# The mixers' gate vector moves from TensorE products to VectorE sums in a flow-matching block

## The chip, the cores and the metric

One Trainium2 chip, one NeuronCore. The metric is the device time of one execution in microseconds; the median of several runs stands for a kernel. TensorE is called PE below, VectorE DVE, ScalarE ACT, GpSimd POOL and SyncE SP, as the profile has them.

## The reference, cut to what matters

The block runs on 256 context tokens and then on 256 latent tokens, with the same weights, in fp32. A modulation comes first: six vectors of 2048 from a conditioning vector.

```python
def _modulation(cond, w, bias):
    m = jax.nn.silu(cond) @ w + bias
    return [a[:, None, :] for a in jnp.split(m, 6, axis=-1)]
...
o_c, ctx_states = _mix(_modnorm(h_c, norm1_g[l], m_c[0], m_c[1]), h_c.shape[1], zero, lp)
o_x, _ = _mix(_modnorm(h_x, norm1_g[l], m_x[0], m_x[1]), GRID_W, ctx_states, lp)
h_x = h_x + m_x[2] * o_x
h_x = h_x + m_x[5] * _swiglu(_modnorm(h_x, norm2_g[l], m_x[3], m_x[4]), ffn_w_gu[l], ffn_w_down[l])
return _rmsnorm(h_x, final_g)
```

`_mix` is a projection into four groups (GLA, gated delta rule, short convolution, RWKV-7), their scans, and one output projection. Vector 2 of the modulation, `m_x[2]`, is the gate on the mixers' output; vectors 3 and 4 are shift and scale of the second norm; vector 5 is the gate on the feed-forward part. Vector 2 is needed first after the output projection, where the residual is formed.

## The kernel before, in words

Sizes: `D` is 2048, `KT` 16 blocks of 128, `T` 256 tokens. A weight tile in fp32 is loaded as `wraw` (128x512, 256 KB; eight buffers shared by all loads of this kind), and `split` (L253) makes a high part `wh` on ACT and a rest `wl` on DVE; three products per block then give nearly fp32 accuracy. A projection (`proj`, L600) takes one 128-wide column tile of `w_in` in four quarters; each quarter is a load of `wraw`, a split and twelve products into one of the two PSUM banks `big`. `spill` (L628) copies a result into `xs` and writes it to memory as `xr_...`, and `fetch` reads it back where a mixer needs it.

The mixers' middle part is written as a list of tokens, `ORDER` (L41): a lower-case token is the context pass, an upper-case token the latent pass. `rw` is an RWKV unit, `gd` a delta-rule head, `gl` a GLA pair; `pr`, `pd`, `pg` are projections that are spilled for them; `sc` is a short convolution, with three projections of its own; `FF` empties the list `feed`, and `YY` ends the RWKV part. Units of two streams run beside each other: RWKV (tiles `rw_...`, `iva...`, banks `ea`, `la`) and the rest (`gd_...`, `ivb...`, banks `eb`, `lb`). A scheduler lays out each engine's order: what is ready goes by priority, which is the place in the program plus the number behind a token; loads under `high_priority()` go ahead of all that isn't. A tile waits for a buffer of its tag; a load that finds no `wraw` free waits until the earliest reader is done. So the projections, which depend on little, fill PE where the scans leave it free.

There are 66 projections in the list. After `YY0` come 24 of them, in the order `PG1` (6), `PG0` (6), `SC0` (3), then `GL0` and `GL1` (none) and `SC2`, `SC3`, `SC1` (9). `YY0` itself (L1465) closes the pools of RWKV, `iva`, `rw` and `rings`, and opens the pool `yp` in their place, with `reuse_waits="tile"`: a tile of `yp` can be written when the RWKV tiles at its address have been read for the last time. `yp` holds 32 tiles of 1 KB a partition (`yH`, `yL`), and then, in order of first use, `g2` (8 KB), `yr`, `ss` and `prt`. RWKV unit 3 of the latent pass (`RW3`) is the last to use the old tiles.

Vectors 2 to 4 of the modulation are formed by `ada_pieces` (L285): 16 pieces and a finish per vector, put into `feed` at L1434 in the order 3, 4, 2. `proj` takes one piece out of `feed` at each even quarter (L610). A piece loads four tiles `wraw` of `ada_w` (L298) and issues sixteen products into the bank `ob`, with the conditioning vector `sc` as stationary operand of 32 columns. For vector 2 the finish (L308) loads the bias, adds it, and writes the gate to `gate_dram`. After the mixers, `gate_bc` (L498) reads it into `g2` on all partitions, and `residual` multiplies with it.

Vector 5 is formed in the feed-forward part in another way: `gate_piece` (L1557) loads a tile, and DVE multiplies it by the scalar `sc[:, kt, 0:1]` and adds it to `gacc`; a product with a matrix of ones sums the partitions.

Of the kernel before, what the change touches and what calls it, by code (L numbers as in the profile page):

```python
# [16 lines left out]
P = 128  # L17
D = 2048
KT = D // P
# [21 lines left out]
ORDER = ("rw0:-50 pd3 pd2:550 pd1 gd0:650 pg0 gd1 pg1:-150 XX0 rw1 gl0 gd3 rw3 gd2:500 gl1:400 "  # L41
         "rw2:-150 PD0 PR0:-200 XX1 GD0:-100 RW0:50 PR1 PD3 PD1:150 RW1 FF0:-100 PR2:350 PR3:-750 "
         "GD1 RW2 PD2:-1100 GD2:200 RW3 YY0:-450 GD3 PG1 PG0:-350 SC0:-250 GL0:50 GL1:-150 "
         "SC2:-3400 SC3:150 SC1").split()
LEVS = (16, 32, 64)

TILES = ([("small", 0)] + [(n, i) for n, k in (
# [109 lines left out]
def _pack_ada(w):  # L157


    a = w.reshape(KT, P, 6, KT, P)  # L160
    first = a[:, :, 0:2].transpose(3, 1, 0, 2, 4).reshape(KT * P, KT * 2 * P)
    later = w[:, 2 * D:5 * D].reshape(KT, P, 3, 4, 4, P).transpose(2, 4, 0, 1, 3, 5).reshape(3 * 4 * KT * P, 512)
    last = w[:, 5 * D:].reshape(KT * P, 4, 512).transpose(1, 0, 2).reshape(4 * KT * P, 512)
    later = np.concatenate([later, last])
    return np.ascontiguousarray(first), np.ascontiguousarray(later)


# [8 lines left out]
def block_kernel(ctx: ExitStack, tc: tile.TileContext, x, cx, ada_first, ada_later, ada_b, w_in, w_early, w_out,  # L176
                 w_gu, w_down, final_g, consts, params, small, out):
    nc = tc.nc
    V, A, G, TE = nc.vector, nc.scalar, nc.gpsimd, nc.tensor
# [8 lines left out]
    def mk(pool, shape, tag, bufs=None, dt=F32):  # L188
        pool = sub.get(tag[:3], pool) if pool is sub.get("mx") else pool
        return pool.tile(list(shape), dt, tag=tag, name=nm(tag), bufs=bufs)  # L190
# [10 lines left out]
    def tt(o, a, b, op, e=None):  # L201
        (e or V).tensor_tensor(out=o, in0=a, in1=b, op=op)  # L202

    def ts(o, a, s1, op0, s2=None, op1=None, e=None):
        if s2 is None:
            (e or V).tensor_scalar(out=o, in0=a, scalar1=s1, scalar2=None, op0=op0)
        else:
            (e or V).tensor_scalar(out=o, in0=a, scalar1=s1, scalar2=s2, op0=op0, op1=op1)

    def stt(o, a, s, b, op0, op1, e=None):  # L210
        (e or V).scalar_tensor_tensor(out=o, in0=a, scalar=s, in1=b, op0=op0, op1=op1)

    def mm(o, l, r, start=True, stop=True):
        return TE.matmul(o, l, r, start=start, stop=stop)  # L214
# [7 lines left out]
    MUL, ADD, SUB, MIN, MAX = ALU.mult, ALU.add, ALU.subtract, ALU.min, ALU.max  # L222
# [7 lines left out]
    ones = mk(keep, [P, P], "ones")  # L230
# [14 lines left out]
    sc = mk(keep, [P, KT, 32], "sc")  # L245
# [4 lines left out]
    def wraw():  # L250
        return mk(wp[0], [P, wp[1]], "wraw", wp[3])
# [31 lines left out]
    gate_dram = mk(dram, [1, D], "gated")  # L283

    def ada_pieces(ci, bank_of, tmp):  # L285

        st = {}

        def run(j, k0):

            if not st:
                st["ps"] = bank_of([P, 512])
            ps, raws = st["ps"], {}
            for kt in (k0 + 1, k0 + 2, k0 + 3, k0):
                with tc.high_priority():
                    raws[kt] = wraw()
                    r0 = (((ci - 2) * 4 + j) * KT + kt) * P
                    nc.sync.dma_start(raws[kt], ada_later[r0:r0 + P, :])  # L298
            with tc.high_priority():
                for kt in range(k0, k0 + 4):  # L300
                    rv = raws[kt].rearrange("p (g c) -> p g c", g=4)
                    for g in range(4):
                        mm(ps[32 * g:32 * g + 32, j * P:(j + 1) * P], sc[:, kt, :], rv[:, g], kt == 0, kt == KT - 1)

        def finish():
            ps = st["ps"]
            row = wraw()
            if ci == 2:  # L308
                G.memset(row, 0.0)
                for g in range(4):  # L310
                    nc.sync.dma_start(row[32 * g:32 * g + 1, :], ada_b[0:1, ci * D + g * 512: ci * D + (g + 1) * 512])
                tt(row, ps, row, ADD)
                for g in range(4):
                    nc.sync.dma_start(gate_dram[0:1, g * 512:(g + 1) * 512], row[32 * g:32 * g + 1, :])
                return
            acopy(row, ps)
            pt = bank_of([P, 4, 4, 32])
            for b in range(4):
                TE.transpose(pt[:, b].rearrange("p a c -> p (a c)"), row[:, b * P:(b + 1) * P], ident)
            t = modB if ci == 3 else modA  # L320
            tt(t[:, 2, :].rearrange("p (g b) -> p g b", b=4), pt[:, :, :, 0].rearrange("p b g -> p g b"),
               pc("adab", ci * 16, 16).rearrange("p (g b) -> p g b", b=4), ADD)
            if ci == 4:
                stt(t[:, 2, :], t[:, 2, :], 1.0, pc("n2g", 0, 16), ADD, MUL)

        return [lambda j=j, k0=k0: run(j, k0) for j in range(4) for k0 in range(0, KT, 4)] + [finish]

    def rstd_of(src, tmp, n):
        junk = mk(tmp, [P, D], "junk", 1)
# [60 lines left out]
    with ExitStack() as st:  # L390
# [37 lines left out]
        acc = [mk(ps0, [P, 2, T], f"acc{i}") for i in range((NE + 1) // 2)]  # L428
# [36 lines left out]
        w = early_weights(0)  # L465
        ins = first_vectors(0)
        for kt in range(KT):
            wh, wl = w
            if kt < KT - 1:
                w = early_weights(kt + 1)  # L470
# [45 lines left out]
    with mix:  # L516
# [78 lines left out]
                L.append(l)  # L595
            return H, L

        feed = []

        def proj(nHL, which):  # L600

            r0 = TIDX[which] * P
            H, L = nHL
            ps = PB([P, T], "big")
            for hf in range(4):
                with tc.high_priority():
                    raw = wraw()
                    nc.sync.dma_start(raw, w_in[r0:r0 + P, hf * 512:(hf + 1) * 512])
                    wh, wl = split(raw, V)
                if hf % 2 == 0:  # L610
                    for f in feed[:1]:
                        f()
                    del feed[:1]
                for k in range(4):
                    kt = hf * 4 + k
                    a, b = wh[:, k * P:(k + 1) * P], wl[:, k * P:(k + 1) * P]
                    mm(ps, a, H[kt], kt == 0, False)
                    mm(ps, a, L[kt], False, False)
                    mm(ps, b, H[kt], False, kt == KT - 1)
            return ps  # L620
# [263 lines left out]
        def finish(stream):  # L884
            if rest[stream]:
                rest[stream]()
                rest[stream] = None
# [542 lines left out]
        bdLM = Ring(rings, "bdLM", [P, 4, 2, 2, 64], 2)  # L1430
        bdKh = Ring(rings, "bdKh", [P, 4, 2, 64], 1)
        bdE = Ring(rings, "bdE", [P, 4, 2, 64], 1)
        for ci in (3, 4, 2):
            feed += ada_pieces(ci, lambda shape: mk(pb, shape, "ob", 1), mx)  # L1434
        nHL = H0, L0
        rg = None
        for tok in ORDER:
            st, _, ofs = tok.partition(":")
            with tc.high_priority(offset=int(ofs)) if ofs else ExitStack():
                c, low = int(st[-1]), st[:2].lower()  # L1440
                s = int(st[0].isupper())
                if low == "pr":
                    park([(n, c) for n in ("r_k", "r_v", "r_r")[:2 + s] if s or (n, c) not in EARLY], s)
                elif low == "pd":
                    park([(n, c) for n in (dkv, dkv + ("d_q", "d_z"))[s] if s or (n, c) not in EARLY], s)
                elif low == "pg":
                    park(gnames[c] + (gmore[c] if s else []), s)
                elif low == "xx":
                    if c == 0:
                        nHL = load_nT()  # L1450
                        smx = t1("rgate")
                        acopy(smx, proj(nHL, ("small", 0)))
                    else:
                        sms[1] = smalls(smx)
                        prg = pcol(nHL, "r_g", 0)
                        rg, tmp = t1("rgate"), t1("gd_k")
                        logsig(rg, prg, tmp)
                        act(rg, rg, AF.Exp)
                elif low == "ff":
                    for f in feed:  # L1460
                        f()
                    del feed[:]
                elif low == "sc":
                    short_conv(c, nHL)
                elif low == "yy":  # L1465
                    finish("a")
                    rws.close()
                    yp = mix.enter_context(tc.tile_pool(name="yp", bufs=1, reuse_waits="tile"))
                    yH, yL = ([mk(yp, [P, T], f"y{n}{i}", 1, F32R) for i in range(16)] for n in "HL")
                    yt += [yH, yL]  # L1470
                else:
                    dict(gd=gd, rw=rw, gl=gl)[low](c, s)
        finish("b")
# [83 lines left out]
    def gate_piece(i):  # L1557
        kt, q = divmod(i, 4)
        raw = mk(narrow[0], [P, 512], "wraw", narrow[3])
        r0 = ((3 * 4 + q) * KT + kt) * P  # L1560
        nc.sync.dma_start(raw, ada_later[r0:r0 + P, :])
        if kt == 0:
            ts(gacc[q], raw, sc[:, 0, 0:1], MUL)
        else:
            stt(gacc[q], raw, sc[:, kt, 0:1], gacc[q], MUL, ADD)

    gate_todo = list(range(4 * KT))
    for f in range(FT):
# [112 lines left out]
```

## Time and profile before

| | |
|---|---|
| median of 3 runs | 1982.04 us (1973.36 to 1990.49) |
| the profiled execution | 1979.17 us |
| its span, first to last instruction | 1977.4 us |
| PE, PE weight load, DVE, ACT, POOL busy | 94%, 82%, 68%, 52%, 8% of the span |
| granted PE clock, mean | 0.983 |
| mixers' part (list of tokens) | about 159 to 1137 us |
| output projection and second norm | about 1118 to 1230 us |

The span is the profiled execution's own; 1.8 us of its time lie outside. Busy times of PE are modelled ends of pipelined products, so the start of one product to the start of the next is the better measure of what one costs.

### The profile page before, as it was taken

Reading aid. Unit: us, or ns where it says so; the run is one execution under the profiler, and the core shown is the slowest. Engines: PE = TensorE matmul, PEld = TensorE weight load, DVE = VectorE, ACT = ScalarE, POOL = GpSimd, SP = SyncE. Lnnn points to the kernel's source line nnn. Section 1 sums busy time; section 2 is a strip of 40 time slices with the busy share of each in tenths; the row PEclk is TensorE's granted clock in tenths of the full one; section 3 lists DMA queues with packets and bytes.
Section 4 is the critical chain, followed back from the end, with each engine's and each line's share of the span. In section 5 each row is a group of like instructions: output and inputs, shape, how many; then the busy total and the mean of one; then the engine's idle time right before and its main releaser. Section 6 shows DMA issues by size and latency. Waiting matters only on the chain.

```text
span 1977.4 us, 36172 instructions
## 1 busy us (share of the span) xinstructions
PE 1858.0 (94%) x13312; PEld 1622.9 (82%) x13312; DVE 1352.5 (68%) x3327; ACT 1020.7 (52%) x2125; POOL 155.0 (8%) x207
## 2 busy tenths in 40 slices
PE   5898899899999999999999998999999999999998
PEld 3777788788888988888999986888888888888886
DVE  3446767888879789899767567986555555555554
ACT  2225555575575655656455555555555545544444
POOL 0001000000001001101010001110010010000000
PEclk6999999899999999999999999999999999999999
DMA  8985877255473431322344665996555555665664
GB/s 332 397 341 199 277 244 238 69 190 176 126 240 106 146 100 61 101 72 86 110 142 143 220 185 173 318 316 212 184 189 184 189 185 187 201 207 193 193 196 153
DMA packets 162081, 374.66 MB, mean 189 GB/s; under 512 B 17896, under 2 KB 43752, under 8 KB 156784
## 3 DMA queue, kind: packets, MB, share of 16 engines
q1 hardware_dynamic: 156288, 368.21, 55.7%
q10 hardware_dynamic: 5616, 4.14, 0.7%
q8 instruction: 104, 1.70, 0.3%
q14 instruction: 73, 0.60, 0.1%
HBM read 360.48 MB, written 11.80 MB: 188 GB/s over the span
## 4 chain that ended last, share of the span: by engine, by line
PE 75%; DVE 9%; DMA 8%; ACT 5%; issue 2%; POOL 0%; SPq 0%; ACTq 0%; DVEq 0%; POOLq 0%
PE acc L214 40%; PE big L214 14%; PE la L214 6%; DMA wraw<-in_ada_later 5%; PE ea L214 5%; PE lb L214 3%; DVE wl L202 3%; PE eb L214 3%; PE ob L214 2%; ACT wh L197 2%; PE pt L214 0%; DMA wraw<-in_x 0%; DMA xin<-in_cx 0%; ACT rw_z L193 0%; DMA wraw<-in_w_in 0%
## 5 line engine op out<-in xcount | busy, mean ns | idle before, releaser
L202 DVE TENSOR_TENSOR wl<-wraw,wh 128x512 fp32r<-128x512 f32 x856 | 570.7, 693 | 370.0 <-ACT wh L197 364.0
L197 ACT ACTIVATE wh<-wraw 128x512 fp32r<-128x512 f32 x856 | 509.9, 625 | 485.9 <-PE acc L214 197.0
L214 PE MATMUL acc<-n,wh 128*128 128x512 f32 x1408 | 492.7, 398 | 3.3 <-ACT wh L197 3.3
L214 PE MATMUL acc<-n,wl 128*128 128x256 f32 x1408 | 383.2, 282 | 1.8 <-DVE wl L202 1.8
L214 PE MATMUL big<-nh,wh 128*128 128x256 f32 x1056 | 311.9, 296 | 4.4 <-ACT xs L197 3.0
L214 PE MATMUL big<-nh,wl 128*128 128x256 f32 x1056 | 311.2, 295 | 0.7 <-DVE wl L202 0.7
L214 PEld LDWEIGHTS acc<-n,wh 128*128 128x128 f32 x1408 | 259.4, 189 | 60.1 <-ACT wh L197 3.6
L214 PE MATMUL big<-nl,wh 128*128 128x256 f32 x1056 | 307.7, 292 | 0.0
L214 PEld LDWEIGHTS acc<-n,wl 128*128 128x128 f32 x1408 | 267.1, 190 | 11.7 <-DVE wl L202 3.3
L214 PEld LDWEIGHTS big<-nh,wh 128*128 128x128 f32 x1056 | 200.9, 190 | 11.3 <-ACT xs L197 3.8
L214 PEld LDWEIGHTS big<-nh,wl 128*128 128x128 f32 x1056 | 200.5, 190 | 4.0 <-issue 2.1
L214 PEld LDWEIGHTS big<-nl,wh 128*128 128x128 f32 x1056 | 200.8, 190 | 2.0 <-issue 1.1
L214 PE MATMUL acc<-wh,hH 128*128 128x512 f32 x352 | 137.6, 391 | 0.0
L214 PE MATMUL acc<-wh,hL 128*128 128x512 f32 x352 | 137.2, 390 | 0.0
L214 PE MATMUL acc<-wl,hH 128*128 128x512 f32 x352 | 137.2, 390 | 0.0
L202 POOL TENSOR_TENSOR hL<-sg,hH 128x256 fp32r<-128x256 f32 x44 | 46.7, 1061 | 452.5 <-ACT hH L197 452.5
L214 PEld LDWEIGHTS acc<-wh,hH 128*128 128x128 f32 x352 | 66.1, 188 | 14.1 <-ACT up L197 0.2
L214 PEld LDWEIGHTS acc<-wl,hH 128*128 128x128 f32 x352 | 66.1, 188 | 13.9 <-DVE wl L202 0.2
L214 PEld LDWEIGHTS acc<-wh,hL 128*128 128x128 f32 x352 | 66.1, 188 | 13.8
L214 PE MATMUL ob<-wraw,sc 128*32 128x128 f32 x1536 | 52.7, 280 | 24.9 <-DMA wraw<-in_ada_later 21.2
L214 PEld LDWEIGHTS ob<-wraw,sc 128*32 128x32 f32 x1536 | 39.9, 111 | 34.2 <-DMA wraw<-in_ada_later 27.6
L202 DVE TENSOR_TENSOR wl<-wr,wh 128x1408 fp32r<-128x1408 f32 x16 | 26.0, 1624 | 43.3 <-ACT wh L197 43.3
(482 smaller groups left out, 3175.3 us busy)
## 6 DMA issues: line engine op xcount, KB each, us to landing
wraw<-in_w_gu SPq DMA_DIRECT2D x174, 512.0 KB, 3.3
wraw<-in_w_in SPq DMA_DIRECT2D x264, 256.0 KB, 3.2
wraw<-in_ada_later SPq DMA_DIRECT2D x256, 256.0 KB, 4.2
wraw<-in_w_down SPq DMA_DIRECT2D x88, 512.0 KB, 4.2
ad<-in_ada_first SPq DMA_DIRECT2D x32, 1024.0 KB, 9.8
wraw<-in_w_out SPq DMA_DIRECT2D x64, 256.0 KB, 2.8
wr<-in_w_early SPq DMA_DIRECT2D x16, 704.0 KB, 6.2
xin<-in_cx SPq DMA_DIRECT2D x2, 1024.0 KB, 7.9
```

The source lines that it names most:

```text
L197: A.activation(o, i, AF.Copy)
L202: (e or V).tensor_tensor(out=o, in0=a, in1=b, op=op)
L214: return TE.matmul(o, l, r, start=start, stop=stop)
```

## The change

The gate vector (2) leaves `ada_pieces`; shift and scale stay there. Its weights are packed in the layout that vector 5 has, in column quarters of 512. A list `late` of 68 pieces (for each of four quarters, 16 of one load and one DVE operation each, and a finish) is put into `feed` at `YY0`, when `yp` is open; from there on `proj` takes a piece at every quarter, not at every second. The accumulator of a quarter is a tile `prt` of `yp`, with two buffers. The finish multiplies by ones into a bank of `big`, loads the bias row, adds and writes 512 elements of `gate_dram`. `ada_sum` is shared with vector 5. `ORDER` gets a last token `FF0`.

```diff
-         "SC2:-3400 SC3:150 SC1").split()
+         "SC2:-3400 SC3:150 SC1 FF0").split()
...
-    later = w[:, 2 * D:5 * D].reshape(KT, P, 3, 4, 4, P).transpose(2, 4, 0, 1, 3, 5).reshape(3 * 4 * KT * P, 512)
-    last = w[:, 5 * D:].reshape(KT * P, 4, 512).transpose(1, 0, 2).reshape(4 * KT * P, 512)
-    later = np.concatenate([later, last])
+    def quarters(lo, hi):
+        return w[:, lo * D:hi * D].reshape(KT * P, 4 * (hi - lo), 512).transpose(1, 0, 2).reshape(-1, 512)
+
+    later = w[:, 3 * D:5 * D].reshape(KT, P, 2, 4, 4, P).transpose(2, 4, 0, 1, 3, 5).reshape(2 * 4 * KT * P, 512)
+    later = np.concatenate([quarters(2, 3), later, quarters(5, 6)])
...
-            if ci == 2:
-                G.memset(row, 0.0)
-                for g in range(4):
-                    nc.sync.dma_start(row[32 * g:32 * g + 1, :], ada_b[0:1, ci * D + g * 512: ci * D + (g + 1) * 512])
-                tt(row, ps, row, ADD)
-                for g in range(4):
-                    nc.sync.dma_start(gate_dram[0:1, g * 512:(g + 1) * 512], row[32 * g:32 * g + 1, :])
-                return
...
+    def ada_sum(acc, raw, kt):
+        if kt == 0:
+            ts(acc, raw, sc[:, 0, 0:1], MUL)
+        else:
+            stt(acc, raw, sc[:, kt, 0:1], acc, MUL, ADD)
+
+    def gate_pieces(bank_of, tmp):
+
+        st = {}
+
+        def piece(q, kt):
+            if kt == 0:
+                st["acc"] = mk(tmp, [P, 512], "prt", 2)
+            with tc.high_priority():
+                raw = wraw()
+                r0 = (q * KT + kt) * P
+                nc.sync.dma_start(raw, ada_later[r0:r0 + P, :])
+            ada_sum(st["acc"], raw, kt)
+
+        def finish(q):
+            ps = bank_of([P, 512])
+            mm(ps, ones, st["acc"])
+            row = wraw()
+            nc.sync.dma_start(row[0:1], ada_b[0:1, 2 * D + q * 512:2 * D + (q + 1) * 512])
+            tt(row[0:1], ps[0:1, :], row[0:1], ADD)
+            nc.sync.dma_start(gate_dram[0:1, q * 512:(q + 1) * 512], row[0:1])
+
+        return [f for q in range(4) for f in [lambda q=q, kt=kt: piece(q, kt) for kt in range(KT)] +
+                [lambda q=q: finish(q)]]
...
-        feed = []
+        feed, late = [], []
...
-                if hf % 2 == 0:
+                if hf % 2 == 0 or late:
...
-        for ci in (3, 4, 2):
+        for ci in (3, 4):
...
                     yt += [yH, yL]
+                    late += gate_pieces(lambda shape: mk(pb, shape, "big", 2), yp)
+                    feed += late
...
-        if kt == 0:
-            ts(gacc[q], raw, sc[:, 0, 0:1], MUL)
-        else:
-            stt(gacc[q], raw, sc[:, kt, 0:1], gacc[q], MUL, ADD)
+        ada_sum(gacc[q], raw, kt)
```

## Rows read from the trace of the kernel before

**Rows 1.** The page's busy time of each engine over the span.
```profile
PE 1858.0 (94%) x13312; PEld 1622.9 (82%) x13312; DVE 1352.5 (68%) x3327; ACT 1020.7 (52%) x2125; POOL 155.0 (8%) x207
```

**Rows 2.** Busy time by stretch, all instructions: stretch, its length, then the engines.
```profile
core 0: us, PE busy (x) PEld busy (x) DVE busy (x) ACT busy (x) POOL busy (x), PEclk, DMA share, GB/s
352.00:365.00 13.00, 10.04 (x62) 9.27 (x61) 9.98 (x27) 6.30 (x15) 0.00 (x0) 0.77 0.14 41
465.00:610.00 145.00, 135.41 (x1405) 121.13 (x1405) 116.07 (x364) 86.26 (x196) 11.93 (x22) 0.99 0.59 186
895.00:972.00 77.00, 75.30 (x576) 69.96 (x577) 65.94 (x201) 42.78 (x94) 6.18 (x9) 1.00 0.24 75
972.00:1137.00 165.00, 160.46 (x1189) 149.78 (x1188) 108.32 (x223) 90.89 (x189) 11.60 (x10) 1.00 0.53 173
```

**Rows 3.** The same view for the tile ob alone (gate products): PE, PEld, DVE, ACT.
```profile
465.00:610.00 145.00, 17.49 (x512) 13.29 (x512) 0.07 (x1) 0.00 (x0) 0.99 0.59 186
```

**Rows 4.** PE's waits between 465 and 610: us in total, times, longest.
```profile
PE ob L214 <- DMA wraw<-in_ada_later: 3.8, 4, 1.9
```

**Rows 5.** Timeline of PE, 1722 to 1736: the ones products of vector 5.
```profile
1724.42 1.88 PE L214 MATMUL acc<-wh,ones 128*128 128x512 f32 x4
1726.14 1.88 PE L214 MATMUL acc<-wl,ones 128*128 128x512 f32 x4
1727.45 0.80 PE L214 MATMUL acc<-wh,hH 128*128 128x512 f32 x1
```

**Rows 6.** Tile wh, feed-forward part: vector 5's sums (ns min/median/max, first and last start).
```profile
L211 DVE SCALAR_TENSOR_TENSOR wh<-wraw,sc,wh x30: 734/744/1228, 1234.7 to 1339.8; 128x512 f32<-128x512 f32 x30
...
L206 DVE TENSOR_SCALAR wh<-wraw,sc x2: 474/480/486, 1233.3 to 1236.9; 128x512 f32<-128x512 f32 x2
```

**Rows 7.** Timeline of SP: the spills of PG1's projections, and PG0's first.
```profile
871.40 0.38 SPq L633 DMA_DIRECT2D xr_g_k<-xs  x1
...
894.14 0.33 SPq L633 DMA_DIRECT2D xr_g_v<-xs  x1
...
963.40 0.33 SPq L633 DMA_DIRECT2D xr_g_r<-xs  x1
...
978.43 0.33 SPq L633 DMA_DIRECT2D xr_g_k<-xs  x1
```

**Rows 8.** Tiles rw_vt (last reader of the old tiles) and g (columns as in rows 6).
```profile
L214 PE MATMUL la<-rw_Ah,rw_vt x64: 217/274/324, 655.0 to 969.7; 128*128 128x64 f32 x64
...
L499 SPq DMA_DIRECT2D g<-gated x1: 383/383/383, 978.8 to 978.8; - x1
...
L202 DVE TENSOR_TENSOR prt<-big,g x4: 680/682/683, 1158.3 to 1186.9; 128x512 f32<-128x512 f32 x4
```

**Rows 9.** Groups of instructions, 895 to 972: count, busy us, mean ns.
```profile
L214 PE MATMUL big<-nh,wl 128*128 128x256 f32 x68 | 20.6, 303 | 0.0
...
L202 DVE TENSOR_TENSOR wl<-wraw,wh 128x512 fp32r<-128x512 f32 x18 | 12.4, 687 | 1.3 <-ACT wh L197 1.1
```

**Rows 10.** The chain that ended last, 1050 to 1100: one run of projection products.
```profile
1086.75 6.05 PE big L214 x49
```

**Rows 11.** The same chain, 895 to 975, by line.
```profile
by line: PE la L214 22.1%; PE big L214 16.7%; PE lb L214 14.0%; PE eb L214 8.6%; PE ea L214 8.5%; DVE wl L202 3.2%; issue 3.1%; ACT rw_z L193 2.3%; ACT wh L197 1.5%; ACT ivaQ L197 1.3%; POOL rw_sq L208 1.2%; DVE rw_kp L202 1.2%; PE ea L987 
```

**Rows 12.** Tile ob: the products and the finish of the gate vector.
```profile
L214 PE MATMUL ob<-wraw,sc x1536: 272/273/423, 163.1 to 593.0; 128*32 128x128 f32 x192
...
L202 DVE TENSOR_TENSOR wraw<-ob,wraw x1: 692/692/692, 609.9 to 609.9; 128x512 f32<-128x512 f32 x1
```

## The prediction

> **What bounds the kernel now.** I read the page first. PE is busy for 94% of the span, DVE for 68% [rows 1]: over the whole, work taken off PE should be worth about its length, and DVE has room. That is an average, so the second view is the busy time by stretch [rows 2], for the two stretches that the change touches. Between 465 and 610 us, where the gate's products stand, PE is busy 135.4 of 145 and DVE 116.1. In the last third of the projections, 972 to 1137, PE has 160.5 of 165, DVE 108.3. Between them, from 895 to 972, both are nearly full: PE 75.3 and DVE 65.9 of 77. Third come the times at which the last projections run [rows 7] and at which the space for the new accumulators comes free [rows 8]. They decide this case, because the change ties a load that goes ahead early to a tile that is free late.
>
> **The change part by part.**
>
> *Gate products removed.* A third of `ob`'s 1536 records [rows 12] belong to the gate: 512, 17.5 us of PE [rows 3]. PE also waited 3.8 us for their loads [rows 4]. Both go: −21 us, if PE is what sets the pace there. It nearly is, with 135.4 of 145 [rows 2]; the bounds are 0 (only projections move forward and the scans do not) and −27 (PE's other idle, 9.6 us of the 145, shrinks by the share of the products too). I take −21 as what PE gains at this place. The 64 loads of 256 KB leave this stretch, with no further gain that I count.
>
> *Products with ones added.* Vector 5 has the same four: from 1724.42 to the next product at 1727.45, eight records, 3.0 us [rows 5]. In a stretch where PE is 97% busy they cost their length: +3.
>
> *Sums added.* 60 multiply-adds of 744 ns and 4 multiplies of 480 ns [rows 6] are 46.6 us of DVE. Beside the 108.3 us of 972 to 1137 [rows 2] that gives 155 of 165. DVE stays just under PE, so PE's work hides the sums, but not for nothing: behind each one queue the scans' short operations and the `wl` of the next quarter, for which PE waits. Bounds: 0, and +15, a third of the sums uncovered, about what is left if DVE must also keep the idle share that it has between 895 and 972 (11 of 77). I take +4.
>
> *Finish.* Before, the sum stood in a bank of its own, and from the last product at 593.0 to the end of the bias sum at 610.6 [rows 12] that bank was held. Now one of the two banks of `big` is held while a bias row waits for a `wraw` and its load. For that long, projections have one bank, and each must be evicted before the next begins. Bounds 0 and four times some 5 us; I take +2. The gate itself is late for nobody: its 68 pieces end with the 17th projection, while `g2` is first multiplied at 1158.3 [rows 8].
>
> *The wait that is added.* The accumulator is a `prt` of `yp`, which takes the place of RWKV's tiles. In order of first use it is now the first after the 32 KB of `yH` and `yL`, at the address that `g2` had; counting tile sizes, that is on `rw_v`, `rw_vt` and `rw_kt`. The last reader of `rw_vt` starts at 969.7, and the load of `g2`, which waits for nothing else after 610, was issued at 978.8 [rows 8]. But `PG1`'s projections, which bring the first 24 pieces, run from before 871 to 963 [rows 7], ahead of that time. A piece's load goes at high priority, takes a `wraw`, and holds it until its sum has run; the sum cannot run before about 970. Loads of weights and of pieces alternate, so after eight quarters all eight `wraw` hold gate pieces. Then no projection can load its weights: `PG1` stops after two of six, at about the second spill, 894 [rows 7], and the scans lose the work that filled PE between their steps. Queued behind the blocked tile are the sixteen remaining quarters of `PG1`, then `PG0`; SP's other loads, and DVE's scan operations, go ahead as they are ready.
>
> The price: 18 quarters were split between 895 and 972, with 68 products of each of three kinds [rows 9], 202 in all at 0.123 us from start to start (49 in 6.05 us [rows 10]): 25 us of PE that move behind 970, where PE is full. Against that, the scans run freer in the meantime. Of their chain, `big`, `wl` and `wh` make 16.7, 3.2 and 1.5% [rows 11], of 80 us some 17 us, which is the most that they can shorten. I take 14, since DVE's own 53.5 us (65.9 less 12.4) and PE's 50 must still alternate: net +11. Bounds +8 and +25. At the end of the block DVE has eight pieces to work off, 6 us, before buffers come free and loads run again: +2 (0 to +6). And as projections run ahead by what PE gained at 465 to 610, the block begins earlier against the scans: of the 21 us I count 8 as idled away (0 to 21).
>
> [...] The scans' products go on all through the block, so by the row of 352 I would expect a clock of 0.8 to 1.0, and add nothing to the sum; at 0.77 throughout, 50 us of products would become 65, which belongs to the second rival below.
>
> *The sum.* −21 + 3 + 4 + 2 + 11 + 2 + 8 = +9. From the profiled execution's 1979.17 us (span 1977.4 and 1.8 outside it) this is 1988.2. That execution lies 2.9 us under the median of 1982.04, within the spread of the runs (17 us), and I do not correct for it.
>
> **The rivals.**
>
> *A: no block, faster.* The accumulators come free before the pieces need them, or the pieces' loads do not crowd out the weights. Then the terms of the block go: −21 + 3 + 4 + 1 = −13, 1966 us. For it: DVE's order is laid out by readiness, and a different placement of `prt` would suffice. Against: `g2`, at the same address, was not loaded before 978.8 [rows 8]. It decides if `PG1` still spills about every 18 us up to 963. If DVE hides everything and the other idle shrinks too, −24: 1955.
>
> *B: the scans do not use the freed engines, slower.* One mechanism, in the stretch from `PG1`'s second spill to the last read of `rw_vt`: the scans go at the pace of their own round trips among PE, DVE and ACT, so taking projections away shortens nothing, and the gain from 465 to 610 is idled away in full. Then −21 + 21 + 25 + 2 + 3 + 4 + 2 = +36, 2015 us. It decides once the scans shorten by less than about 10 us in all. For it: 2.3% of the chain in this stretch is one ACT operation, `rw_z`, and more are small waits [rows 11]; a lower clock pushes the same way. Against: PE's products are some 70% of that chain.
>
> *C: DVE becomes the bound in the last third.* There is no block, but the sums delay the GLA scan, which has only `SC` behind it to fill PE: −21 + 3 + 15 + 2 = −1, 1978 us. For it: 155 of 165; against: `wout`'s products can begin before GLA ends.
>
> **How the numbers follow.** The forecast has 0.45, A 0.22, B 0.18, C 0.15. A measurement of this kernel can tell about 1% from no change: faster is under 1962, slower over 2002. The forecast, ±20 by its bounds, gives 0.04, 0.31 and 0.10 to faster, same and slower; A 0.11, 0.11, 0; B 0, 0.03, 0.15; C 0.02, 0.12, 0.01. Together 0.17, 0.57, 0.26. The predicted time is the forecast's, 1988. The range goes down to 1961, which leaves out the better half of A, and up to 2012, which leaves out the worse half of B and little else.
>
> **What would show it.** Right: 512 `ob` records and their waits gone before 610, and PE some 15 to 20 us ahead of its old schedule there; the spills of `PG1` stop after the second for 50 us or more; the first sum stands just behind the last read of `rw_vt`, eight of them close together; PE has visible gaps before, and projections are packed behind; DVE over 90% busy in the last third. Wrong: first sums well before the end of `RW3`, or `PG1` spilling evenly (A or C); `RW3` ending as late as before in spite of the block (B). If `residual` waits for `g2`, the finish was mispriced.

## The result, and the profile after

| | before | after |
|---|---|---|
| median | 1976.07 us (6 runs, 1973.36 to 1990.49) | 2000.97 us (6 runs, 1997.74 to 2004.03) |
| ratio of the means | | 1.0111, 95% interval 1.0079 to 1.0143 |
| profiled execution, its span | 1979.17, 1977.4 us | 1997.74, 1996.0 us |
| granted PE clock, mean | 0.983 | 0.984 |

The kernel became slower by 22 us (0.0111 of some 1977), or 18.6 by the two profiled executions. That is clear of no change, though small. The rows of after are read in the order of the prediction. The line numbers moved by a few: 214 is 216 now, 633 is 657, 211 is 213.

The page's busy time of after. Against [rows 1], PE has 505 instructions and 6 us less and DVE has 42 us more: the work moved as planned.

```profile
PE 1852.0 (93%) x12807; PEld 1612.8 (81%) x12808; DVE 1394.4 (70%) x3394; ACT 1021.6 (51%) x2125; POOL 155.5 (8%) x206
```

Busy time by stretch of after (columns as in [rows 2]; the first stretch is one of [rows 2], the others follow the block).

```profile
465.00:610.00 145.00, 136.75 (x1044) 126.62 (x1042) 126.99 (x407) 94.74 (x217) 14.92 (x23) 0.99 0.28 89
871.00:938.00 67.00, 53.63 (x347) 43.78 (x346) 52.31 (x175) 29.03 (x65) 6.10 (x9) 0.95 0.04 12
938.00:1040.00 102.00, 81.53 (x599) 76.29 (x600) 78.34 (x139) 42.17 (x84) 3.37 (x3) 0.94 0.84 264
1040.00:1084.00 44.00, 40.30 (x306) 36.97 (x306) 37.83 (x77) 23.92 (x53) 4.43 (x4) 0.99 0.67 207
```

Between 465 and 610 PE is as busy as before with 361 products fewer; the short products of the gate are gone and longer ones have moved up. From 871 to 938 PE stands idle for 13.4 of 67 us and the DMA engines are almost empty, a share of 0.04. In the next 102 us PE is idle for another 20.5, with the DMA at 0.84.

The timeline of SP in after, the loads and spills around that hole (start, length, what). Lines 632 and 338 are the loads of weights and of gate pieces.

```profile
850.16 0.40 SPq L657 DMA_DIRECT2D xr_g_k<-xs  x1
...
858.17 0.33 SPq L338 DMA_DIRECT2D wraw<-in_ada_later  x1
...
871.29 0.32 SPq L657 DMA_DIRECT2D xr_g_v<-xs  x1
...
938.73 0.33 SPq L632 DMA_DIRECT2D wraw<-in_w_in  x1
...
940.06 0.33 SPq L338 DMA_DIRECT2D wraw<-in_ada_later  x1
...
952.90 0.38 SPq L657 DMA_DIRECT2D xr_g_v<-xs  x1
...
989.00 0.60 SPq L657 DMA_DIRECT2D xr_g_q<-xs  x1
```

The load at 858.17 is the eighth of a piece (the first is at 788.48). Behind it no weight and no piece is loaded for 80 us, and `PG1` spills once more, at 871.29, and then not for 82 us. The first weight follows at 938.73.

Tiles of after: the last reader of the old space, the sums, and the residual (columns as in [rows 6]).

```profile
L216 PE MATMUL la<-rw_Ah,rw_vt x64: 217/275/323, 636.8 to 931.3; 128*128 128x64 f32 x64
```

```profile
L208 DVE TENSOR_SCALAR prt<-wraw,sc x4: 478/480/486, 938.2 to 1030.2; 128x512 f32<-128x512 f32 x4
L213 DVE SCALAR_TENSOR_TENSOR prt<-wraw,sc,prt x60: 731/746/1772, 939.3 to 1076.0; 128x512 f32<-128x512 f32 x60
L204 DVE TENSOR_TENSOR prt<-big,g x4: 679/680/681, 1175.7 to 1204.3; 128x512 f32<-128x512 f32 x4
```

The first sum stands at 938.2, half a microsecond before the first weight load and 6.9 us behind the start of the last product with `rw_vt`. Against [rows 8] the last read of `rw_vt` comes 38.4 us earlier, and yet the residual comes 17.4 us later, which is nearly all of the 18.6.

Two markers cut this into parts that can be compared between kernels: `PG1`'s first spill (871.40 before [rows 7]) and the last read of `rw_vt`. The first marker belongs to the projections, and the scans can stand earlier or later at that moment. So a third is taken from the scans themselves, the last `rw_bonus`, an early step of `RW3`. Its rows before, after, and in the second experiment:

```profile
L202 DVE TENSOR_TENSOR rw_bonus<-ea,rw_v x4: 409/417/418, 608.3 to 903.9; 128x256 f32<-128x256 f32 x4
L204 DVE TENSOR_TENSOR rw_bonus<-ea,rw_v x4: 415/417/425, 591.8 to 871.0; 128x256 f32<-128x256 f32 x4
L204 DVE TENSOR_TENSOR rw_bonus<-ea,rw_v x4: 411/418/425, 593.2 to 882.3; 128x256 f32<-128x256 f32 x4
```

All figures are differences of rows like those above; `RW3` stands for the stretch from that step to the last `rw_vt`.

| us | first spill | from it to the last `rw_vt` | of this, `RW3` | from the last `rw_vt` to the residual | first spill to residual |
|---|---|---|---|---|---|
| before | 871.4 | 98.3 | 65.8 | 188.6 | 286.9 |
| after | 850.2 | 81.1 | 60.3 | 244.4 | 325.5 |
| no gate (first experiment) | 847.4 | 88.2 | 64.6 | 195.4 | 283.6 |
| pieces from `PG0` (second) | 849.8 | 98.3 | 65.8 | 203.8 | 302.1 |
| the same, loads only | 847.1 | 98.3 | 65.8 | 193.9 | 292.2 |
| the same, sums only | 851.2 | 98.3 | 65.8 | 201.6 | 300.0 |
| after, accumulator in PSUM | 839.6 | 120.0 | 77.0 | 196.7 | 316.7 |
| after, loads at low priority | 846.8 | 79.9 | 59.1 | 232.6 | 312.5 |
| after, spill write on POOL | 854.6 | 91.9 | 59.7 | 240.5 | 332.4 |
| after, spill write on ACT | 849.1 | 93.4 | 60.1 | 239.0 | 332.4 |

The column `RW3` tells what the block does to the scans. In this stretch PE has 165 products of projections (bank `big`) before and none after, and the same number for the RWKV unit (173 of bank `la`); the other stream has 78 of bank `lb` and 66. Without the projections the stretch takes 60.3 us instead of 65.8. So of the 17.2 us by which the second column is shorter in after, the block explains some 5.5. The other 11.7 come from where the scans stand: the step follows the first spill after 32.5 us before and after 20.8 in after, and after 23.6 in the kernel without the gate, in which nothing blocks. Why the scans stand further ahead there isn't shown.

### The profile page after: what moved, and what is told of

Read it like the earlier page. It is cut to its first block, busy times and chain, and to the rows that moved or that the text cites. A ratio compares the mean times of both kernels' runs of the same rounds, so it can differ in the third digit from the quotient of the medians.

```text
span 1996.0 us, 35241 instructions
## 1 busy us (share of the span) xinstructions
PE 1852.0 (93%) x12807; PEld 1612.8 (81%) x12808; DVE 1394.4 (70%) x3394; ACT 1021.6 (51%) x2125; POOL 155.5 (8%) x206
## 4 chain that ended last, share of the span: by engine, by line
PE 70%; DVE 12%; DMA 9%; ACT 6%; issue 2%; POOL 0%; SPq 0%; DVEq 0%; ACTq 0%; POOLq 0%
PE acc L216 38%; PE big L216 12%; DMA wraw<-in_ada_later 6%; PE la L216 5%; PE ea L216 5%; DVE wl L204 4%; PE lb L216 4%; PE eb L216 3%; ACT wh L199 2%; PE ob L216 1%; DMA ad<-in_ada_first 1%; DVE prt L213 1%; DMA wraw<-in_w_in 1%; ACT rw_z L195 0%; PE pt L216 0%
## 5 line engine op out<-in xcount | busy, mean ns | idle before, releaser
L216 PEld LDWEIGHTS acc<-n,wl 128*128 128x128 f32 x1408 | 267.0, 190 | 11.8 <-DVE wl L204 3.2
L213 DVE SCALAR_TENSOR_TENSOR prt<-wraw,sc,prt 128x512 f32<-128x512 f32 x60 | 45.8, 763 | 18.2 <-DMA wraw<-in_ada_later 17.7
L216 PE MATMUL acc<-nh,wh 128*128 128x256 f32 x176 | 50.6, 295 | 2.4 <-ACT nh L199 2.4
```

## The experiments

The theory after this reading: the removal brings what was predicted, and the price is the block, that is, loads that take all eight `wraw` ahead of a tile that is free late. Rivals: DVE is full with the sums; the loads' DMA traffic costs; the loads' priority is to blame, not the place of the accumulator. A microsecond worked out from a ratio below is a difference of ratios times 1977. The kernels ran on several chips, so ratios to the kernel before on the same chip are compared, not medians.

**What the removal is worth.** The kernel before, without vector 2's products:

```diff
-        for ci in (3, 4, 2):
+        for ci in (3, 4):
...
+        for g in range(4):
+            row = wraw()
+            nc.sync.dma_start(row[0:1], ada_b[0:1, 2 * D + g * 512:2 * D + (g + 1) * 512])
+            nc.sync.dma_start(gate_dram[0:1, g * 512:(g + 1) * 512], row[0:1])
```

> The kernel before without the gate vector's 64 loads and 256 products: the gate is the bias alone, and nothing takes the products' place. This measures the first term of the prediction by itself, at minus 21 us: 1953 to 1960 where before is 1976 to 1980. If the products were hidden behind the scans (the lower bound of the term), 1972 to 1980.

Measured 1954.36 us, ratio 0.9878 (0.9851 to 0.9905): −24 us, between −19 and −29 by the interval. The first spill is 24.0 us early and the rest of the way is 3.3 us shorter.

**No block: pieces begin with PG0.** The list `late` is put into `feed` one token later. The edit also changes a second thing: with `or feed`, the pieces of shift and scale are taken at every quarter too. The last of them ends at 314.0 here and at 468.4 in after (the rows behind the edit).

```diff
-                if hf % 2 == 0 or late:
+                if hf % 2 == 0 or feed:
...
                 elif low == "pg":
+                    if s == 1 and c == 0:
+                        feed += late
...
-                    feed += late
```

```profile
L204 DVE TENSOR_TENSOR modA<-ob,par x1: 176/176/176, 314.0 to 314.0; 128x16 f32<-128x16 f32 x1
L204 DVE TENSOR_TENSOR modA<-ob,par x1: 167/167/167, 468.4 to 468.4; 128x16 f32<-128x16 f32 x1
```

> The pieces begin six projections later, with PG0's first, so PG1's weights no longer stand behind loads that wait for the accumulator. Theory (the block of the eight wraw by pieces whose accumulator is not free, then a rebuild of the lead of the weights' loads, cost about 45 us): PG1 spills evenly again, PE is over 95% busy until the last read of rw_vt, and the time falls from the changed kernel's 1998 to 1966 to 1982. Rival (the scans and the order of the tokens set the pace, the block is idle time that costs nothing): 1993 to 2003, though the spills are even. Rival (the sums on DVE and the doubled loads in the last third cost the most): 1990 to 2000, with PE below 90% between 970 and 1100.

Measured 1974.01 us, ratio 0.9974 (0.9962 to 0.9987). The time is as the theory had it. The distance to after's 1.0111 is far outside both intervals: 0.0137, 27 us, which is the block's price if the second thing is worth nothing (the first spill, 849.8 against 850.2, shows no gain from it). In the timeline of SP of this kernel `PG1` spills evenly again:

```profile
849.75 0.38 SPq L657 DMA_DIRECT2D xr_g_k<-xs  x1
872.47 0.33 SPq L657 DMA_DIRECT2D xr_g_v<-xs  x1
...
910.74 0.33 SPq L657 DMA_DIRECT2D xr_g_q<-xs  x1
...
941.73 0.33 SPq L657 DMA_DIRECT2D xr_g_r<-xs  x1
```

and its busy time in the two stretches that after lost is that of a full PE, at a granted clock of 1.00:

```profile
871.00:938.00 67.00, 64.42 (x486) 59.35 (x485) 60.23 (x183) 40.18 (x88) 5.27 (x6) 1.00 0.25 78
938.00:1040.00 102.00, 95.22 (x707) 86.97 (x706) 85.90 (x178) 49.62 (x108) 10.97 (x12) 1.00 0.70 221
```

Pieces wait for the accumulator here as well: the first is loaded at 900.77, and the first sum stands at 958.1. But only five are loaded up to the last read of `rw_vt` (948.1) and seven up to that sum, so the weights keep buffers; `PG0`'s first spill comes at 956.85, no later than the 958.21 of the kernel with sums only, which loads no pieces.

```profile
L208 DVE TENSOR_SCALAR prt<-wraw,sc x4: 473/480/482, 958.1 to 1062.8; 128x512 f32<-128x512 f32 x4
```

Yet the kernel is 19 us slower than the one without the gate (0.9974 less 0.9878), where the prediction had 9 for everything that is added. By the table 10.1 of 18.5 us lie ahead of the last `rw_vt` and of the first sum (98.3 against 88.2), where this kernel agrees with before; they come from where the scans stand and can't be a cost of sums in the last third. The next two take the rest apart.

**Loads without sums, sums without loads.** Both from the kernel that begins with `PG0`. The first:

```diff
-            ada_sum(st["acc"], raw, kt)
+            if kt == 0:
+                V.memset(st["acc"], 0.0)
```

> As e1 (pieces from PG0 on), with the 64 sums left out: the pieces' loads land and nobody reads them, the accumulators are zeros, the products with ones and the finish stay. The gate is the bias alone. e1 lies 19 us above e3, which has none of the gate's work. Theory (DVE's sums cost most of it): 1957 to 1963. Rival (the loads cost it: eight wraw and SP's queue are shared by twice as many loads): 1966 to 1974.

The second:

```diff
-            with tc.high_priority():
-                raw = wraw()
...
-            ada_sum(st["acc"], raw, kt)
+            ada_sum(st["acc"], sw[:, 2048:2560], kt)
```

> As e1, with the pieces' 64 loads left out: the same 64 sums read a tile that is resident, so the gate's values are others. Theory (DVE's sums): 1966 to 1974, as e1. Rival (the loads and the wraw that they hold): 1957 to 1963. If each alone is cheap and both together are not, both stand near 1960.

Loads alone: 1965.77 us, ratio 0.9942 (0.9924 to 0.9959), 13 us above the kernel without the gate and between the two forecasts. Sums alone: 1972.83 us, 0.9983 (0.9967 to 1.0000), 21 us above it, as with both together (19). These three figures can't be added up: each holds the ones products, the finishes, the denser pieces of shift and scale, and the 98.3 us ahead of the first sum. The kernel before is the better base for the last third, as it too has 98.3 there, and behind the last `rw_vt` PE has 1300 products in it and 1307 or 1308 in these three. Against its 188.6 us, loads only takes 5.3 more, sums only 13.0, and both take 15.2. The first two exceed the third by 3.1, about the ones products (3.0 [rows 5]), which both hold. So in the profiled executions loads and sums add up: the sums cost 9.9 us, the loads 2.2. By the ratios the sums cost 6 us beside the loads, and the loads nothing that can be measured beside the sums.

Busy time from 960 to 1100 of four kernels, first without the gate:

```profile
960.00:1100.00 140.00, 134.69 (x1030) 126.89 (x1029) 92.67 (x191) 75.92 (x157) 9.59 (x8) 1.00 0.49 156
```

loads only:

```profile
960.00:1100.00 140.00, 134.41 (x1033) 125.79 (x1032) 94.42 (x201) 75.19 (x159) 10.04 (x9) 1.00 0.75 240
```

sums only:

```profile
960.00:1100.00 140.00, 127.12 (x969) 118.88 (x968) 128.79 (x248) 71.07 (x152) 10.26 (x9) 0.99 0.43 139
```

and both:

```profile
960.00:1100.00 140.00, 129.07 (x967) 119.54 (x966) 125.62 (x238) 70.36 (x145) 9.36 (x8) 0.99 0.81 260
```

With the sums DVE goes from 93 to 126 or 129 of 140 us (90 to 92%) and PE loses 6 to 8. With the loads alone, at nearly as high a DMA share, PE loses 0.3. So the sums hold PE up in this stretch and the loads do not.

**The accumulator elsewhere.** After, with the accumulator in the PSUM bank `ob`, which is free by then; there is one accumulator instead of two, and the finish copies it to a `wraw` first.

```diff
-                st["acc"] = mk(tmp, [P, 512], "prt", 2)
+                st["acc"] = mk(tmp, [P, 512], "ob", 1)
...
+            col = wraw()
+            acopy(col, st["acc"])
             ps = bank_of([P, 512])
-            mm(ps, ones, st["acc"])
+            mm(ps, ones, col)
```

> The accumulator is the PSUM bank ob, which nobody uses after the shift and scale are formed, instead of a tile on RWKV's space; the finish copies it to a wraw first. The pieces stay where they are, from PG1 on. Theory (only the late accumulator blocks): sums run from PG1's first quarter on, about 800 us, no stop in PG1's spills, 1964 to 1980. Rival (eight wraw shared by weights and pieces are too few wherever the pieces stand): PE stays under 92% busy while pieces are loaded, 1985 to 2000. DVE's operation gets longer or shorter by the PSUM operand; by 0.1 us it would be 6 us of DVE.

Measured 1977.91 us, ratio 0.9994 (0.9979 to 1.0009). This has the same pieces at the same place with the same priority as after; the wait on the RWKV tiles is gone, and with it 23 us. The time is as the theory had it. The tile `ob` there, and two spills of `PG1`:

```profile
L208 DVE TENSOR_SCALAR ob<-wraw,sc x4: 748/752/754, 802.4 to 1017.4; 128x512 f32<-128x512 f32 x4
L213 DVE SCALAR_TENSOR_TENSOR ob<-wraw,sc,ob x60: 743/750/757, 807.0 to 1059.1; 128x512 f32<-128x512 f32 x60
...
877.32 0.33 SPq L659 DMA_DIRECT2D xr_g_v<-xs  x1
...
916.56 0.33 SPq L659 DMA_DIRECT2D xr_g_q<-xs  x1
```

The work begins at 802.4, and a multiply-add took 750 ns against 746 in SBUF. But the theory's "no stop" did not come true: the fourth spill follows the third after 39 us, and only 17 of the 64 operations start before 936. Pieces now wait for DVE, which was nearly full beside the end of the scans before [rows 2]; 22 of its operations of this kind fall into `RW3`, which takes 77.0 us instead of 65.8. So what it saves behind the scans (196.7 us against 203.8 from `PG0`) is paid here.

**The loads' priority.** After, without the high priority of the pieces' loads.

```diff
-            with tc.high_priority():
-                raw = wraw()
+            raw = wraw()
...
```

> The changed kernel with one edit: the pieces' loads go at the place's own priority, not ahead with the weights. Theory (pieces' loads that go ahead take the wraw away from the weights): weights go first, PG1 spills evenly again while pieces take what is left, 1968 to 1985. Rival (any piece that holds a wraw until the accumulator is free blocks in the end, whatever its priority): PG1 stops again after a few spills, 1993 to 2003.

Measured 1987.47 us, ratio 1.0050 (1.0034 to 1.0066), between the two forecasts. The block stays, as the rival had it: spills at 846.82 and 867.96, the third at 949.13, and from 895 to 960

```profile
895.00:960.00 65.00, 51.93 (x344) 45.23 (x344) 49.84 (x137) 24.26 (x52) 4.51 (x6) 0.92 0.32 97
```

Eight pieces are loaded by 854.83 and the ninth at 936.10, as in after. So the priority is not what makes the block; the pieces take the buffers without it too. Still, 12 us are gained, and by the table above 11.8 of the profiled difference (15.6) lie behind the last read of `rw_vt`: the restart is better. The same edit on a kernel without a block:

```diff
-            with tc.high_priority():
...
```

> e1 (pieces from PG0 on) with the same edit as e7, the pieces' loads at the place's own priority. No piece waits for its accumulator for long here, so the edit shows what loads ahead cost without the block. e7 gained 12 us by it against the changed kernel. If that gain came from the alternation of weights and pieces after the block: 1960 to 1968. If it came from the block itself (pieces took the buffers later): 1971 to 1977, as e1.

Measured 1974.27 us, ratio 0.9971 (0.9954 to 0.9988), the same as 0.9974. Without a block the priority is worth nothing. (Pieces do wait for their accumulator here, from 900.98 to 958.3, against what the expectation says.)

**Why the restart is slow.** In after, between 938 and 1090, the sums wait for their loads sixteen times, and the longest single waits of PE and ACT hang on `xs`, the buffer of a spill (us in total, times, longest):

```profile
DVE prt L213 <- DMA wraw<-in_ada_later: 17.7, 16, 2.6
...
PEld big L216 <- ACT xs L199: 9.8, 1, 9.8
...
PE big L216 <- ACT xs L199: 9.6, 1, 9.6
ACT xs L199 <- DMA xr_g_v<-xs: 7.7, 1, 7.7
```

ACT had written that `xs` at 962.65, but SP issued its write to memory only at 989.00, behind loads that waited for buffers. Two edits let another engine issue it, POOL in after and, as a control, in the kernel that begins with `PG0`:

```diff
-            nc.sync.dma_start(dst, t)
+            nc.gpsimd.dma_start(dst, t)
```

> The changed kernel with one edit: the write of a spilled projection is issued by POOL, not by SP, so it no longer stands behind SP's loads of weights and pieces. Theory (after the block the restart loses some 10 us because the writes of PG1's projections wait in SP's queue behind loads that wait for buffers, so that the two xs stay taken): PE's wait of 9.6 us on xs goes, the fourth spill of PG1 comes within 15 us of the third instead of 36, and the time is 8 to 12 us below the changed kernel's, about 1.005 of before. Rival (the restart is slow because weights and pieces share eight buffers and DVE must sum in between; the late write is a by-product): the wait moves to the weights and the time stays at 1.010 to 1.012. Both expect the block itself (PG1 stopping after two spills until about 938) to stand.

> The kernel whose pieces begin with PG0 (no block, ratio 0.9974), with the same edit: spill writes issued by POOL. Control for what that queue is worth without a block. Theory: nothing, 0.996 to 0.999. Rival (spill writes are late behind loads everywhere in the last third): it gains 3 us or more, below 0.996.

Measured: 2005.94 us, ratio 1.0126 (1.0098 to 1.0155), and for the control 1987.48 us, 1.0043 (1.0029 to 1.0056). In the first, the fourth spill comes 9.6 us after the third (969.05 and 978.66) and not 36, as the theory had it, but the time did not follow. The time lies above both forecasts, and both missed the control, which lost 14 us. POOL now waits for the copies, 65.6 us in nine waits by the three rows below, between 938 and 1090 in the first of the two:

```profile
POOL xr_g_r L657 <- ACT xs L199: 39.0, 4, 15.8
...
POOL xr_g_q L657 <- ACT xs L199: 13.4, 2, 9.0
...
POOL xr_g_v L657 <- ACT xs L199: 13.2, 3, 6.9
```

That the scans pay for these waits, since their own operations on POOL stand behind them, was only argued: in the control the longest sum of waits for POOL, DVE's for POOL's `rw_sq`, is 4.7 us between 159 and 1160, against 6.7 without the edit. The cause of the 14 us stays open.

So the edit brought a cost of its own wherever it comes from, and ACT, which has just made the copy, was tried in its place (`A.dma_start`):

> The changed kernel with the write of a spilled projection issued by ACT, the engine that has just written xs, instead of SP or POOL. On POOL the write stood in line with the scans' own work; behind its own copy on ACT it should hold up little. The block (PG1 stopping after two spills until the end of RW3) stays under both theories. Theory (the late writes in SP's queue cost the restart some 10 us): the write follows its copy within 2 us, no wait of PE or ACT on xs is left, the stretch from PG1's first spill to the residual shrinks from 325.5 us by 8 or more, and the ratio is 1.004 to 1.007. Rival (the restart is bound by the shared load buffers and DVE, the late write is a by-product): that stretch stays within 4 us of 325.5 and the ratio at 1.009 or above.

Measured 2004.85 us, ratio 1.0136 (1.0106 to 1.0165). The write now follows its copy within half a microsecond, PE's wait on `xs` fell from 9.6 to 1.9 us, and the kernel is not faster. The late write as a cost of some 10 us has fallen. The rival had the ratio right and the stretch from first spill to residual wrong by 3 (332.4). The table shows where the time went: `RW3` is as short as in after (60.1 and 59.7 against 60.3), and behind it both kernels are shorter than after, by 5.4 and 3.9 us. But their scans stand 12.5 and 11.4 us further back at the first spill (33.3 and 32.2 us to the step of `RW3`, against 20.8). The edit moves every spill write from the context pass on, so this can be its own cost; it isn't shown how. What gave 12 us to the kernel with low priority stays open too: its scans stand as in after, and its gain lies in the restart.

**Fewer sums at a time.** From the kernel with the PSUM accumulator: pieces from the first `FF0` on, at every second quarter, so that 34 projections carry them and not 17.

```diff
-                if hf % 2 == 0 or late:
+                if hf % 2 == 0:
...
                     del feed[:]
+                    if not late:
+                        late += gate_pieces(lambda shape: mk(pb, shape, "big", 2), pb)
+                        feed += late
```

> As e2 (accumulator in the bank ob), with the pieces begun at FF0 instead of YY0 and taken at every second quarter: 34 projections for 68 pieces, half as dense. Theory (what costs is two loads through eight wraw per quarter, with weights only four quarters ahead): 1958 to 1972, faster than e1. Rival (DVE, 87% busy from 465 to 970, has no room for 47 us of sums before the last third): 1975 to 1990.

Measured 1968.25 us, ratio 0.9947 (0.9927 to 0.9968). This is faster than before by 10 us and than after by 32, and within the theory's range. Against the kernel from `PG0` the gain, 5 us, is at the edge of the noise (0.9962 to 0.9987 there). With low priority as well:

> e6 (accumulator in the bank ob, pieces from FF0 on at every second quarter) with the pieces' loads at the place's own priority, behind the weights. If what is left of e6's loss against e3 (0.9947 to 0.9878 of before, some 14 us) is weights waiting behind pieces' loads: 1958 to 1965. If it is DVE's 47 us of sums in stretches where DVE is over 85% busy: 1965 to 1972, as e6.

Measured 1973.12 us, ratio 0.9961 (0.9948 to 0.9974), 1 us above both forecasts: no gain from that. Of the 24 us that the removal is worth, 10 are kept at best; DVE from 610 to 895 is then busy for 269.95 of 285 us, so that no stretch of the mixers' part is left with much room for sums:

```profile
610.00:895.00 285.00, 270.92 (x2041) 248.72 (x2040) 269.95 (x838) 173.57 (x383) 32.56 (x47) 1.00 0.36 112
```

## Why the prediction was right, and where it was not

The prediction was slower by 9 us; measured were 18.6 in the profiled executions, 22 by the ratio. The time lies within the range, on the slower side, and the mechanism is the one forecast. In the forecast's three parts, by the table: −21 for the removal was −21.2 at the first spill; +9 for what is added in the last third was +15.2; +21 for the block was +23.4 (325.5 against 302.1). That makes 17.4 at the residual. The terms below these sums were partly wrong, some of them against each other.

- *Gate products, −21.* Right: the first spill is 21.2 us early in after, and the kernel without them is 24 us faster. The choice of the PE time and PE's waits was near the truth; the bound of −27 lies within the interval of that run.
- *The block itself.* Right in each step: eight pieces hold all eight `wraw`, `PG1` stops after two of six spills, for 82 us and not only 50, and loads begin again half a microsecond after the first sum. The kernel with the accumulator in PSUM shows that it is the place of the accumulator, and the one with low priority that "a piece's load goes at high priority" was not needed for it. Which of `RW3`'s tiles is the last that the first sum waits for isn't shown; it stands behind `RW3`'s last operations, 6.9 us after the last `rw_vt`.
- *The block's price, 11 + 2 + 8 = 21.* That the total came near is luck, for only one term in it was right. That term is the deferred work: between the first spill and the last `rw_vt` PE has 249 products of projections in the block-free kernel and 48 in after, 201 fewer, where 202 were counted (25 us). But the scans were to shorten by 14 of 80 us when these products go; `RW3` shortened by 5.5 of 65.8. In its 60.3 us PE then idles for 11.5, so the scans go mostly at a pace of their own. Of the early gain nothing was idled away, where 8 was taken: the scans end 38.4 us early. The restart cost far more than its +2: from 938 to 1040 PE is idle for 20.5 us in after and 6.8 in the block-free kernel, 13.7 more. That the buffers come free one by one, each behind a sum, and that weights and pieces then alternate for the same eight, was foreseen for the eight first pieces only; in after, from 938 to 1090, loads of weights wait 10.4 us for sums (20 waits) and 11.2 us for `wl` (25), loads of pieces 9.1 us (22) and 10.0 us (17). And no term had the 11.7 us by which the scans stand further ahead at the first spill than in the block-free kernel; they are in the 23.4 too.
- *What is added in the last third, 3 + 4 + 2 = 9.* This is the step that failed by size: 15.2 without any block. Ones products, finishes and loads take 5.3, where 5 was taken, with nothing for the loads. The sums take 9.9 (6 by the ratios), where 4 was taken. "PE's work hides the sums, but not for nothing" was too kind: 46.6 us of DVE were right (60 at a median of 746 ns, 4 of 480), but DVE at 90% takes 6 to 8 us from PE between 960 and 1100 alone. The bound of +15 holds.
- *Rival C*, DVE as the bound in the last third, was set up as an alternative to the block. It is partly true beside it: the sums cost more than the forecast's 4, and less than the 15 given here. Its time, 1978, is within 0.3% of the kernel that begins with `PG0`, which is the case that it described. *Rival A* needed that the sums be free, and no kernel came near 1966 with all sums in the last third. *Rival B* fell, as the scans ended 38.4 us early and the early gain was not idled away. Its mechanism, scans that go at the pace of their own round trips, was nearer to the 5.5 us than the forecast's 14.
- *The clock.* Granted were 0.95 and 0.94 in the two stretches of the block, where PE was busy for 53.6 of 67 and 81.5 of 102 us, within the 0.8 to 1.0 given; in the same two stretches of the kernel that begins with `PG0`, with PE busy for 64.4 and 95.2 us, it was 1.00. A price can't be read off: PE took 0.136 us of busy time a product from 938 to 1040 and 0.135 in the block-free kernel, but not of the same products. The 65 us for 50 at 0.77 were the author's estimate, in proportion to the clock; no run shows that price, and neither stretch of the block stood at 0.77 as a whole.
- *What would show it.* The signs of the block all came. DVE over 90% in the last third did not: it had 77% from 938 to 1040 and 86% from 1040 to 1084, since the restart starved it too. It reached 90% only in the kernels without a block. The residual does not wait for `g2`, whose load is issued at 1088.8. The finish holds its bank for some 2.7 us, from the ones product at 965.18 to the end of the addition, rather than the 5 assumed.

## What to carry to other kernels

When a load shares its buffers with the main stream, look up when its *consumer* can run, not when the load can: one tile that comes free late closed eight buffers and cost 23 to 27 us, what the change had removed. Work that fills another chain's gaps is worth little to that chain when it goes: 26 us of projections taken out of `RW3` shortened it by 5.5. After such a block, price the restart by itself, since buffers come back at the pace of the consumer that caused it (in the 102 us after it PE was idle for 20.5 us here, against 6.8 without it). And work that is moved to an engine with room on the average (108.3 of 165 us here) can still hold up the first: 46.6 us of sums cost 6 to 10. To compare stretches of two kernels, take a marker from the chain that is meant: a spill of the projections says nothing of where the scans stand.

## What was not expected of the hardware

- Loads of 256 KB, one beside each weight load, cost next to nothing beside the sums: with a DMA share of 0.81 instead of 0.43, 2.2 us by the table and nothing by the ratios.
- Moving the spill writes from SP's queue to another engine's gained nothing, on POOL or on ACT: after went from 1.0111 to 1.0126 with POOL (busy for 8% of the span) and to 1.0136 with ACT (51%), which is within the noise, and the block-free kernel lost 14 us with POOL. ACT was not tried there.
- Taking away the longest single wait in the restart (9.6 us on `xs`) shortened the restart by 4 to 5 us and the time not at all, as the scans stood 11 to 12 us further back.
- A multiply-add with its accumulator in PSUM took 750 ns against 746 in SBUF, so the place of the accumulator was free to choose. The plain multiply, four of the 64, took 752 ns with its result in PSUM and 480 in SBUF.
